# The RWKV stage of a two-layer trunk: VectorE's order written out by hand, substitutions and factors moved to other periods

## The chip, the cores and the metric

One core of a Trainium2 chip runs the whole program. The metric is the device time of one execution in microseconds (us); lower is better. About 0.5% of it, some 16 us, is what a measurement of this kernel can tell from no change.

## What is computed

The reference is a trunk of two layers (an MLA attention and a bidirectional RWKV side by side, then a mixture of experts), followed by a second block. The change touches only the RWKV part. For each of 8 heads and both directions it runs a recurrence over 528 positions with a 64 by 64 state:

```python
def step(S, inp):                       # one position
    r_t, w_t, k_t, v_t, kk_t, b_t = inp # b = kk * a
    sa = einsum('bhvk,bhk->bhv', S, kk_t)
    S = S * w_t[:, :, None, :] - sa[..., None] * b_t[:, :, None, :] + v_t[..., None] * k_t[:, :, None, :]
    return S, einsum('bhvk,bhk->bhv', S, r_t)

decay = exp(-exp(-softplus(-wl) - 0.5)); a = sigmoid(a0[d] + ad @ a2[d])
kd = k * (1 + (a - 1) * k_a)
y = scan(r, decay, kd, v, kk, a, reverse); bonus = sum(r * kd * r_k) * v
out = (group_norm(y_f + y_b) + bonus_f + bonus_b) * g
```

## The kernel before

The 528 positions (padded to 576) are cut into 9 chunks of 64. The work of a layer is 8 units: unit = (pair of heads, direction), two heads on the two halves of the 128 partitions. A unit passes through these steps, each a Python generator whose `yield`s are the places where other work may be put in between:

- **front** (L740): TensorE makes the two small products `sg` and `ta` (L764), ScalarE their tanh; GpSimd `sig` (L771), VectorE a running sum (L773), GpSimd its difference (L774), ScalarE three exponentials (L776 to L778). For a forward unit TensorE and VectorE first scale `kk` (L737, L738).
- **gen** (L787): VectorE multiplies the factors `KR` (L801, L805) and, with GpSimd, `BK` (L802 to L810) and, for a backward unit, the bonus factor (L852, L853); TensorE turns v (L884), makes the matrices Z of all chunks (L827) and turns BK (L842); VectorE masks Z (L830) and a DMA writes its triangular parts to DRAM (`Md`, L836).
- **inv** (L903): a DMA brings the 16 by 16 diagonal blocks back with one block per partition (`rnt`, L909); VectorE inverts them by substitution, 14 rounds of two small instructions (L914, L916); DMAs write the result out (`Td`, L922) and read it back in another layout (`rtb`, L927).
- **kx** (L983): transposes of KR (L884) and a product X (L993).
- **join** (L930): blocks of 16 are joined to 32 and to 64 by four rounds of TensorE and VectorE (L944 to L979). Its result T is what the next unit's solve reads.
- **solve** (L998): the products WC (L1006) and PG (L1017, added up on VectorE in L1018 and L1020), three groups of chunks each.
- **scan** (L1023): E and Y (L1036, L1050), then eight dependent steps, each two matmuls E (L1059), one VectorE scaling that writes the next state (L1060; L1052 before the first), and the output matmuls Y (L1062).
- **post** (L1078), for every finished pair of heads: group norm and gate; VectorE L1096, GpSimd L1102 and L1104, VectorE L1108.

`spread` deals several generators out in proportion to the number of steps that is given for each. `rwkv` (L1110) uses it: a prologue makes units 0 to 2 ready, then eight periods follow, one for each unit's solve and scan (the chain). Period i runs the chain of unit i, the join of unit i+1 inside the scan, and, spread over it, gen(i+2), kx(i+2) with inv(i+2), front(i+3), and in even periods from 2 on the post of an earlier pair.

The region is under `manual_schedule(engines={PE})`: TensorE issues in the order in which the program emits, while the order on VectorE, ScalarE, GpSimd and the DMA queue SP is chosen by a scheduler that works from a modelled timeline. Every engine issues its own queue in order. The pools named `rt`, `rbk`, `rnt` hold 7, 1 and 2 buffers.

Of the kernel before, what the change touches and what calls it, by code (L numbers as in the profile page):

```python
# [26 lines left out]
L = 528  # L27
# [76 lines left out]

# [6 lines left out]
class K:  # L111
# [503 lines left out]
    def rwkv_open(self, n):  # L615

        return (self.popen("rwl", dict(rl=(1, 1))),
                self.open("rwl", "left", dict(ryy=(LP, 2), rpt=(L, 2), rw2=(512, 3))),
                self.popen("rwp", dict(r=(1, 5), re=(1, 1), ry=(1, 1))),
                self.open("rw", "left", dict(  # L620
                    rq=(288, 2), rtb=(256, 3), rt0=(16, n), rtt=(LP, 2), rkx=(2 * LP, 2), rw=(LP, 1), rzb=(3 * LP, 2 * n),
                    rsv=(2 * LP, n), rkr=(2 * LP, n))),
                self.open("rg", "right", dict(rt=(LP, 7), rkk=(LP, 2), rkd=(L, 1), rbk=(2 * LP, 1), rpr=(56, 2), rnt=(256, 2), rsc=(LP, 1))))

# [47 lines left out]
    def rwkv_pre(self, li, u, rn):  # L672
# [67 lines left out]
    def rwkv_front(self, li, S, p, d, G):  # L740

        nc = self.nc
        par = S["par"]
        k = S["k"][p]
        if d == 0:
# [28 lines left out]
        nc.gpsimd.tensor_tensor(out=sig, in0=ai, in1=sig, op=ALU.subtract)  # L774
        eP, eE, eN = (self.t("rt", (128, LP)) for _ in range(3))
        nc.scalar.activation(out=eN, in_=ai, func=AF.Exp, scale=CDEC)  # L776
# [3 lines left out]
        nc.gpsimd.tensor_copy(al, c64(eP)[:, :, 63])  # L780
        G.update(p=p, d=d, al=al, ta=ta, eP=eP, eE=eE, eN=eN)
        yield

    def rwkv_gen(self, li, S, G):

        nc = self.nc
        p, d, ta, eP, eE, eN = (G[x] for x in ("p", "d", "ta", "eP", "eE", "eN"))  # L787
        par = S["par"]
        r, k, v, kk = S["r"][p], S["k"][p], S["v"][p], S["kk"][p]

# [3 lines left out]
        def rev(a):  # L794
            return a[:, :, ::-1] if d else a

        KR = self.t("rkr", (128, 2, NCH, 64))
        BK = S["BK"]
        b2 = self.t("rt", (128, LP))
        nc.vector.scalar_tensor_tensor(out=b2, in0=ta, scalar=1.0, in1=kk, op0=ALU.add, op1=ALU.mult)  # L800
        nc.vector.tensor_tensor(out=KR[:, 0], in0=rev(c64(kk)), in1=c64(eE), op=ALU.mult)  # L801
# [3 lines left out]
        nc.vector.tensor_tensor(out=KR[:, 1], in0=rev(c64(r)), in1=c64(eP), op=ALU.mult)  # L805
        for h in range(2):
            o = OWN[h]
            nc.vector.scalar_tensor_tensor(out=BK[o, :, h], in0=rev(c64(b2))[o], scalar=0.5, in1=c64(eN)[o], op0=ALU.mult,
                                           op1=ALU.mult)
            nc.gpsimd.tensor_tensor(out=BK[o, :, 1 - h], in0=rev(c64(ta))[o], in1=c64(eN)[o], op=ALU.mult)  # L810

        if d:
            vd = self.t("rt", (128, LP))
            nc.scalar.copy(rev(c64(vd)), c64(v))
        else:
            vd = v
# [20 lines left out]
        for c0, n in ((0, 5), (5, 4)):  # L837
# [7 lines left out]
            yield  # L845
        if d == 0:
            S["kd0"] = self.t("rkd", (128, L))
            nc.scalar.copy(S["kd0"], ta[:, PAD:])
        else:

            bs = S["kd0"]
            nc.gpsimd.tensor_tensor(out=bs, in0=bs, in1=ta[:, PAD:], op=ALU.add)  # L852
            nc.vector.scalar_tensor_tensor(out=bs, in0=r[:, PAD:], scalar=self.col(f"rk{li}", p), in1=bs, op0=ALU.mult,  # L853
                                           op1=ALU.mult)
        G.update(KR=KR, Zx=[z[:, :, 0] for z in ZB], BZ=[z[:, :, 1:3] for z in ZB], SV=SV)

    def rwkv_bonus(self, S, G):
        nc = self.nc
        bs, v = S["kd0"], S["v"][G["p"]]
        for c0, n in HALVES:  # L860
# [251 lines left out]
    def rwkv(self, li, u, rn, nb, freed):  # L1112
# [14 lines left out]
        def front(i):  # L1127
            if i <= last:
                yield from self.rwkv_front(li, S, *units[i], G[i])

        def gen(i):
            if i <= last:
                yield from self.rwkv_gen(li, S, G[i])
                inv = self.rwkv_inv(S, G[i])
                next(inv)
                if units[i][1]:
                    yield from self.rwkv_bonus(S, G[i])
                G[i]["inv"] = inv

        def back(i):  # L1140
            if i <= last:
                yield from spread((self.rwkv_kx(G[i]), 5), (G[i]["inv"], 7))
                if i == last:
                    self.close(hg)
                    freed()

        def join(i):
            if i <= last:
                yield from self.rwkv_join(S, G[i])

        def chain(i):
            yield from self.rwkv_solve(S, G[i])
            yield from spread((self.rwkv_scan(S, G[i]), 10), (join(i + 1), 4))

        with self.tc.manual_schedule(engines={ENG.PE}):
            run(spread((itertools.chain(front(0), gen(0), back(0)), 21), (front(1), 2)))
            run(spread((itertools.chain(gen(1), back(1)), 19), (front(2), 2)))
            run(spread((gen(2), 9), (join(0), 4)))
            for i in range(len(units)):
                behind = itertools.chain(gen(i + 2) if i else (), back(i + 2), front(i + 3))  # L1160
                p = i // 2 - 1
                post = self.rwkv_post(li, p, S, "r") if i % 2 == 0 and i else iter(())
                run(spread((chain(i), 20), (behind, 22), (post, 5)))
        self.close(hw)
# [1702 lines left out]
```

## Time and profile before

| | us |
|---|---|
| median of 3 runs | 3232.27 (3231.17 to 3242.57) |
| the profiled execution's own time | 3221.64 |
| its span | 3219.9 |
| RWKV of layer 0 in that span | 283.4 to 647.5 |
| RWKV of layer 1 in that span | 1374.1 to 1739.7 |

The span is what the trace covers; the time also holds what lies around it (1.7 us here). Times in the rows are counted from the span's start. A period begins with the first WC matmul (L1006) of its unit. A bracket at a row's end gives the idle time of that engine just before it and what ended it. PEclk is TensorE's granted clock as a share of 2.4 GHz, so 0.50 is 1.2 GHz.

### The profile page before, as it was taken

The page shows a single profiled execution, that of the slowest core. Times are in us where ns is not written, and L with a number is a line of the kernel's source. Part 1 is how long each engine was busy: PE and PEld are TensorE (multiplying, and loading weights), DVE is VectorE, ACT ScalarE, POOL GpSimd, SP SyncE. Part 2 cuts the span into 40 slices and gives each one's busy share as a digit, 9 for nine tenths or more (in the row PEclk, how much of TensorE's full clock was granted, in tenths as well). Part 3 has the DMA queues.
Part 4 walks back from the last instruction along what each step waited for, and adds up shares of the span by engine and source line. Part 5 has one row for each costly group of instructions (what it writes and reads, how often), then busy time and mean ns, then how long its engine had stood idle before and what let it go on. Part 6 is the DMA issues. An engine that isn't in the chain of part 4 may idle for free. (4 is left out here: it accounts for less than half of the span.)

```text
span 3219.9 us, 54694 instructions
## 1 busy us (share of the span) xinstructions
PE 2735.7 (85%) x21572; PEld 2085.6 (65%) x21572; DVE 1547.5 (48%) x3328; ACT 1086.0 (34%) x2377; POOL 1245.7 (39%) x1276
## 2 busy tenths in 40 slices
PE   6998777887789599967778788769888999999998
PEld 5887655664344288846557543248776788778886
DVE  6565545444124437664544611154867667344412
ACT  3223333311233322233332111144335665244431
POOL 3224222242244332341231511036865543655554
PEclk9997667787899799967778799989899999999999
DMA  5220111137989624311103599942121124523333
GB/s 186 63 86 20 19 16 16 61 133 304 364 344 374 249 69 148 90 29 19 16 13 123 199 361 420 420 173 92 55 76 43 61 71 130 156 87 97 98 119 104
DMA packets 224045, 443.18 MB, mean 138 GB/s; under 512 B 96577, under 2 KB 105153, under 8 KB 197137
## 3 DMA queue, kind: packets, MB, share of 16 engines
q1 hardware_dynamic: 209648, 407.76, 36.4%
q0 software_dynamic: 9216, 25.44, 2.1%
q10 hardware_dynamic: 4912, 6.34, 0.5%
q8 instruction: 175, 2.87, 0.4%
q14 instruction: 94, 0.76, 0.1%
HBM read 400.91 MB, written 46.61 MB: 139 GB/s over the span
## 5 line engine op out<-in xcount | busy, mean ns | idle before, releaser
L225 POOL TENSOR_TENSOR wl<-wr,wh 128x512 fp32r<-128x512 f32 x328 | 438.2, 1338 | 538.0 <-ACT wh L224 502.6
L224 ACT CAST wh<-wr 128x512 fp32r<-128x512 f32 x352 | 217.5, 619 | 552.0 <-PE mm L331 213.1
L330 PE MATMUL mm<-hh,wh 128*128 128x264 f32 x608 | 186.7, 307 | 19.1 <-ACT hf L285 13.0
L330 PE MATMUL mm<-h,wh 128*128 128x512 f32 x480 | 187.6, 391 | 2.5 <-ACT h L224 2.5
L332 PE MATMUL mm<-h,wl 128*128 128x512 f32 x480 | 187.5, 391 | 1.2 <-POOL wl L225 1.2
L331 PE MATMUL mm<-h,wh 128*128 128x512 f32 x480 | 187.4, 391 | 0.4 <-DVE h L225 0.4
L332 PE MATMUL mm<-hh,wl 128*128 128x264 f32 x608 | 181.4, 298 | 0.0
L331 PE MATMUL mm<-hl,wh 128*128 128x264 f32 x608 | 180.0, 296 | 0.0
L1455 POOL DMA_INDIRECT ybuf<-my,rdst x32 | 32.3, 1010 | 277.8 <-DVE my L1454 247.0
L330 PEld LDWEIGHTS mm<-hh,wh 128*128 128x128 f32 x608 | 119.0, 196 | 29.5 <-ACT hf L285 13.5
L330 PE MATMUL go<-h,wh 128*128 128x512 f32 x288 | 121.0, 420 | 11.6 <-ACT th L2139 6.8
L1426 DVE SCALAR_TENSOR_TENSOR mth<-mth,w 128x256 f32<-128x256 f32 x32 | 13.5, 421 | 236.0 <-ACT mth L1425 236.0
L331 PEld LDWEIGHTS mm<-hl,wh 128*128 128x128 f32 x608 | 119.1, 196 | 2.6 <-issue 1.3
L332 PEld LDWEIGHTS mm<-hh,wl 128*128 128x128 f32 x608 | 118.6, 195 | 2.3 <-issue 1.3
L1437 PE MATMUL w<-mw,xT 128*64 128x512 f32 x344 | 113.5, 619 | 5.5 <-DMA mw<-in_moe_w_dram 5.3
L332 PE MATMUL go<-h,wl 128*128 128x512 f32 x288 | 115.6, 401 | 0.0
L331 PE MATMUL go<-h,wh 128*128 128x512 f32 x288 | 115.2, 400 | 0.0
L1059 PE MATMUL E<-rzb,rkr 64*64 64x64 f32 x448 | 46.2, 296 | 80.9 <-DVE rzb L1060 54.5
L771 POOL TENSOR_SCALAR rt<-rt 128x576 f32<-128x576 f32 x16 | 10.8, 678 | 261.7 <-ACT rt L766 215.2
L219 POOL TENSOR_SCALAR rs<-s 128x4 f32<-128x4 f32 (+7 forms) x62 | 14.6, 236 | 236.1 <-DVE s L719 160.7
L330 PEld LDWEIGHTS mm<-h,wh 128*128 128x128 f32 x480 | 90.4, 188 | 21.4 <-ACT h L224 2.6
L332 PEld LDWEIGHTS mm<-h,wl 128*128 128x128 f32 x480 | 90.5, 189 | 20.7 <-POOL wl L225 2.1
(610 smaller groups left out, 7633.3 us busy)
## 6 DMA issues: line engine op xcount, KB each, us to landing
mw<-in_moe_w_dram SPq DMA_DIRECT2D x61, 1024.0 KB
mz<-in_moe_w_dram SPq DMA_DIRECT2D x48, 1024.0 KB
me<-in_moe_w_dram SPq DMA_DIRECT2D x47, 1024.0 KB
wr<-in_w_in_dram SPq DMA_DIRECT2D x176, 256.0 KB
mx<-in_moe_w_dram SPq DMA_DIRECT2D x36, 1024.0 KB
hf<-in_w_mod_dram SPq DMA_DIRECT2D x96, 256.0 KB
wr<-in_w_up_dram SPq DMA_DIRECT2D x88, 256.0 KB
wr<-in_w_down_dram SPq DMA_DIRECT2D x44, 256.0 KB
```

What stands on the lines that cost most here:

```text
L219: nc.gpsimd.tensor_scalar(out=a, in0=b, scalar1=float(mul), scalar2=float(eps), op0=ALU.mult, op1=ALU.add)
L224: self.nc.scalar.copy(hi, src)
L225: lo_eng.tensor_tensor(out=lo, in0=src, in1=hi.bitcast(F32), op=ALU.subtract)
L330: nc.tensor.matmul(out, lhsT=w[0], rhs=x[0], start=start, stop=False)
L331: nc.tensor.matmul(out, lhsT=w[0], rhs=x[1], start=False, stop=False)
L332: nc.tensor.matmul(out, lhsT=w[1], rhs=x[0], start=False, stop=stop)
L771: nc.gpsimd.tensor_scalar(out=rev(c64(sig)), in0=c64(sg), scalar1=0.5, scalar2=0.5, op0=ALU.mult, op1=ALU.add)
L1059: nc.tensor.matmul(o[OWN[h]], lhsT=P[OWN[h], c], rhs=St[OWN[h], c], start=False, stop=True, skip_group_check=True)
L1426: nc.vector.scalar_tensor_tensor(out=th, in0=th, scalar=1.0, in1=p[:, 0:256], op0=ALU.add, op1=ALU.mult)
L1437: nc.tensor.matmul(p1[q], lhsT=xT[:, kt, q], rhs=w13[kt // 4][:, kt % 4], start=kt == 0, stop=kt == 7)
L1455: nc.gpsimd.indirect_dma_start(out=ybuf, out_offset=bass.IndirectOffsetOnAxis(ap=dst, axis=0), in_=y, in_offset=None, bounds_check=2 * L - ...
```

## The change

1. The region's guard becomes `engines={PE, DVE}`: VectorE also issues in the order of emission.
2. Everything of a unit's factors but KR moves from gen to front: the products with `b2`, `ta`, the two halves of BK, the turned v (`vd`) and the bonus factor. They are made for unit i+3 in period i; gen(i+2) begins with KR alone. front gets `yield`s between its steps (8 steps in place of 1 or 2). `rbk` has 2 buffers instead of one shared one, `rt` 8 instead of 7.
3. inv runs a period later: period i holds inv(i+1), in its first third, and join(i+1) in its last 4 ninths. Before, inv(i+2) was in period i and the join in the scan.
4. The prologue is rearranged accordingly: it holds one substitution, inv(0), where before it held those of units 0 and 1.

```diff
-        S["BK"] = self.t("rbk", (128, NCH, 2, 64))      # one buffer, in rwkv_pre
 # rwkv_front: yields added behind sg, ta, sig and the running sum; behind the exponentials, moved from rwkv_gen:
+        nc.vector.scalar_tensor_tensor(out=b2, in0=ta, scalar=1.0, in1=kk, op0=ALU.add, op1=ALU.mult)
+        nc.gpsimd.tensor_scalar(out=ta, ...); nc.gpsimd.tensor_tensor(out=ta, in0=ta, in1=k, op=ALU.mult)
+        yield
+        BK = self.t("rbk", (128, NCH, 2, 64))           # both halves, VectorE and GpSimd; then vd
+        yield
+            nc.gpsimd.tensor_tensor(out=bs, in0=bs, in1=ta[:, PAD:], op=ALU.add)     # if d
+            yield
+            nc.vector.scalar_tensor_tensor(out=bs, in0=r[:, PAD:], scalar=self.col(f"rk{li}", p), in1=bs, ...)
 # rwkv
-        with self.tc.manual_schedule(engines={ENG.PE}):
-            run(spread((itertools.chain(front(0), gen(0), back(0)), 21), (front(1), 2)))
-            run(spread((itertools.chain(gen(1), back(1)), 19), (front(2), 2)))
-            run(spread((gen(2), 9), (join(0), 4)))
+        with self.tc.manual_schedule(engines={ENG.PE, ENG.DVE}):
+            run(front(0))
+            run(spread((gen(0), 8), (front(1), 9)))
+            run(spread((gen(1), 9), (itertools.chain(wait(2), inv(0)), 10), (front(2), 8)))
+            run(spread((gen(2), 8), (itertools.chain(kx(0), kx(1)), 10), (itertools.chain(wait(4), join(0)), 8)))
             for i in range(len(units)):
-                behind = itertools.chain(gen(i + 2) if i else (), back(i + 2), front(i + 3))
-                run(spread((chain(i), 20), (behind, 22), (post, 5)))
+                chain = itertools.chain(self.rwkv_solve(S, G[i]), self.rwkv_scan(S, G[i]))
+                behind = itertools.chain(gen(i + 2) if i else (), kx(i + 2), front(i + 3))
+                run(spread((chain, 17), (behind, 22 if i else 13), (itertools.chain(inv(i + 1), wait(18)), 27),
+                           (itertools.chain(wait(5), join(i + 1)), 9), (post, 5)))
```

`wait(n)` yields n times and does nothing: it only takes up places in the deal.

## Rows read from the trace of the kernel before

**Rows 1.** The page, part 1: busy time, share and instructions of each engine

```profile
PE 2735.7 (85%) x21572; PEld 2085.6 (65%) x21572; DVE 1547.5 (48%) x3328; ACT 1086.0 (34%) x2377; POOL 1245.7 (39%) x1276
```

**Rows 2.** Layer 0 by stretches: prologue, periods 0, 1, 2, 5, 6, 7

```profile
core 0: us, PE busy (x) PEld busy (x) DVE busy (x) ACT busy (x) POOL busy (x), PEclk, DMA share, GB/s
283.40:362.40 79.00, 51.83 (x524) 40.77 (x524) 50.82 (x111) 30.55 (x75) 30.58 (x29) 0.58 0.15 29
362.40:389.60 27.20, 22.34 (x454) 18.28 (x452) 15.64 (x53) 12.14 (x32) 9.92 (x10) 0.75 0.11 15
389.60:433.40 43.80, 34.16 (x523) 26.71 (x522) 20.34 (x66) 12.79 (x37) 0.81 (x2) 0.66 0.10 15
433.40:486.20 52.80, 39.71 (x542) 29.72 (x542) 26.93 (x76) 18.41 (x47) 20.10 (x20) 0.66 0.08 12
...
579.10:614.10 35.00, 26.55 (x509) 21.94 (x510) 16.28 (x59) 9.96 (x31) 6.10 (x5) 0.70 0.23 56
614.10:634.30 20.20, 19.26 (x425) 15.44 (x423) 9.34 (x29) 5.17 (x17) 5.50 (x7) 0.92 0.37 146
634.30:647.50 13.20, 11.30 (x204) 9.79 (x200) 5.35 (x17) 8.53 (x19) 1.05 (x2) 0.88 0.01 1
```

**Rows 3.** What TensorE waited for, layer 0, periods 1 to 7 (us in total, times, longest)

```profile
PE E L1059 <- DVE rzb L1060: 25.0, 22, 5.7
PE E L1059 <- DVE rzb L1052: 11.4, 5, 3.1
PE tok L884 <- ACT rt L814: 7.5, 2, 3.8
PE Z L827 <- POOL rbk L810: 6.8, 4, 2.7
```

**Rows 4.** The same of layer 1, periods 1 to 7

```profile
PE E L1059 <- DVE rzb L1060: 24.4, 24, 5.7
PE E L1059 <- DVE rzb L1052: 15.0, 5, 3.6
```

**Rows 5.** VectorE's queue in order of time, period 1: first product, then a scan step

```profile
408.91 0.17 DVE L914 TENSOR_TENSOR rpr<-rnt 72x14 f32<-72x14 f32 x1 [5.25 <-DMA rnt<-Md]
...
415.99 0.27 DVE L1060 TENSOR_SCALAR rzb<-E,s 128x64 f32<-128x64 f32 x1
...
422.50 0.45 DVE L944 STREAM_TRANSPOSE rq<-rtb 128x256 f32<-128x256 f32 x1 [1.83 <-DMA rtb<-Td]
```

**Rows 6.** TensorE's queue in order of time: scan steps of periods 1 and 7

```profile
416.31 0.48 PE L1059 MATMUL E<-rzb,rkr 64*64 64x64 f32 x4 [5.74 <-DVE rzb L1060]
...
643.59 0.33 PE L1059 MATMUL E<-rzb,rkr 64*64 64x64 f32 x4 [0.27 <-DVE rzb L1060]
```

**Rows 7.** Stretches within period 2: in and after the gap

```profile
460.00:462.00 2.00, 0.48 (x3) 0.49 (x4) 1.79 (x9) 0.00 (x0) 0.00 (x0) 0.50 0.00 0
462.00:480.00 18.00, 16.25 (x234) 11.57 (x234) 7.68 (x26) 4.59 (x12) 3.98 (x5) 0.50 0.10 13
```

**Rows 8.** SP's queue: the write of period 1's inverted blocks

```profile
416.10 1.69 SPq L922 DMA_DIRECT2D Td<-rnt  x2
```

**Rows 9.** GpSimd's queue: a backward unit's factors (period 0), a post (period 2)

```profile
377.86 0.67 POOL L771 TENSOR_SCALAR rt<-rt 128x576 f32<-128x576 f32 x1 [26.46 <-ACT rt L766]
...
388.44 1.30 POOL L852 TENSOR_TENSOR rkd<-rkd,rt 128x528 f32<-128x528 f32 x1
...
469.12 1.18 POOL L1102 TENSOR_SCALAR ryy<-ryy,pv 128x264 f32<-128x264 f32 x1 [13.25 <-DVE ryy L1096]
470.38 0.74 POOL L1104 TENSOR_TENSOR ryy<-ryy,u 128x264 f32<-128x264 f32 x1
```

**Rows 10.** VectorE's queue in the prologue: bonus factor, one substitution step beside GpSimd

```profile
307.97 0.77 DVE L853 SCALAR_TENSOR_TENSOR rkd<-ur,pv,rkd 128x528 f32<-128x528 f32 x1 [1.28 <-POOL rkd L852]
...
340.52 1.42 DVE L916 TENSOR_TENSOR rnt<-rnt,rpr 72x54 f32<-72x54 f32 x1
```

**Rows 11.** GpSimd's queue at that place

```profile
340.46 1.41 POOL L774 TENSOR_TENSOR rt<-rt,rt 128x576 f32<-128x576 f32 x1 [1.88 <-DVE rt L773]
```

More of the change, by code (lines that the diff above doesn't have):

```diff
@@ L102, in spread, with wait @@
             continue
+        yield
+def wait(n):
+    for _ in range(n):
         yield
@@ L743, in rwkv_front @@
         par = S["par"]
-        k = S["k"][p]
+        r, k, v = S["r"][p], S["k"][p], S["v"][p]
         if d == 0:
@@ L780, in rwkv_front @@
         nc.gpsimd.tensor_copy(al, c64(eP)[:, :, 63])
[L781 to L789, printed above, removed]
-        def c64(t):
-            return t.rearrange("p (c t) -> p c t", t=64)
[L794 to L798, printed above, removed]
         b2 = self.t("rt", (128, LP))
+        kk = S["kk"][p]
         nc.vector.scalar_tensor_tensor(out=b2, in0=ta, scalar=1.0, in1=kk, op0=ALU.add, op1=ALU.mult)
-        nc.vector.tensor_tensor(out=KR[:, 0], in0=rev(c64(kk)), in1=c64(eE), op=ALU.mult)
         nc.gpsimd.tensor_scalar(out=ta, in0=ta, scalar1=par[:, 16 + p:17 + p], scalar2=par[:, 20 + p:21 + p],
@@ L804, in rwkv_gen @@
         nc.gpsimd.tensor_tensor(out=ta, in0=ta, in1=k, op=ALU.mult)
-        nc.vector.tensor_tensor(out=KR[:, 1], in0=rev(c64(r)), in1=c64(eP), op=ALU.mult)
+        yield
+        BK = self.t("rbk", (128, NCH, 2, 64))
         for h in range(2):
@@ L816, in rwkv_gen, with c64, rev @@
             vd = v
+        yield
+        if d == 0:
+            S["kd0"] = self.t("rkd", (128, L))
+            nc.scalar.copy(S["kd0"], ta[:, PAD:])
+        else:
+            bs = S["kd0"]
+            nc.gpsimd.tensor_tensor(out=bs, in0=bs, in1=ta[:, PAD:], op=ALU.add)
+            yield
+            nc.vector.scalar_tensor_tensor(out=bs, in0=r[:, PAD:], scalar=self.col(f"rk{li}", p), in1=bs, op0=ALU.mult,
+                                           op1=ALU.mult)
+        G.update(p=p, d=d, al=al, eP=eP, eE=eE, BK=BK, vd=vd, bs=S["kd0"])
+        yield
+    def rwkv_gen(self, li, S, G):
+        nc = self.nc
+        p, d, eP, eE, BK = (G[x] for x in ("p", "d", "eP", "eE", "BK"))
+        r, kk = S["r"][p], S["kk"][p]
+        def c64(t):
+            return t.rearrange("p (c t) -> p c t", t=64)
+        def rev(a):
+            return a[:, :, ::-1] if d else a
+        KR = self.t("rkr", (128, 2, NCH, 64))
+        for i, (x, e) in enumerate(((kk, eE), (r, eP))):
+            nc.vector.tensor_tensor(out=KR[:, i], in0=rev(c64(x)), in1=c64(e), op=ALU.mult)
         SV = self.t("rsv", (128, NCH, 2, 64))
-        yield from self.by_token(vd, SV[:, :, 0], SV[:, :, 1], True)
+        yield from self.by_token(G["vd"], SV[:, :, 0], SV[:, :, 1], True)
         ZB = [self.t("rzb", (128, NCH, 3, 64)) for _ in range(2)]
@@ L845, in rwkv_gen @@
             yield
[L846 to L854, printed above, removed]
         G.update(KR=KR, Zx=[z[:, :, 0] for z in ZB], BZ=[z[:, :, 1:3] for z in ZB], SV=SV)
@@ L858, in rwkv_bonus @@
         nc = self.nc
-        bs, v = S["kd0"], S["v"][G["p"]]
+        bs, v = G["bs"], S["v"][G["p"]]
         for c0, n in HALVES:
@@ L1127, in front @@
         def front(i):
-            if i <= last:
-                yield from self.rwkv_front(li, S, *units[i], G[i])
+            return self.rwkv_front(li, S, *units[i], G[i]) if i <= last else iter(())
         def gen(i):
@@ L1133, in gen, with kx, inv @@
                 yield from self.rwkv_gen(li, S, G[i])
-                inv = self.rwkv_inv(S, G[i])
-                next(inv)
                 if units[i][1]:
                     yield from self.rwkv_bonus(S, G[i])
-                G[i]["inv"] = inv
-        def back(i):
+        def kx(i):
+            return self.rwkv_kx(G[i]) if i <= last else iter(())
+        def inv(i):
             if i <= last:
-                yield from spread((self.rwkv_kx(G[i]), 5), (G[i]["inv"], 7))
+                yield from self.rwkv_inv(S, G[i])
                 if i == last:
@@ L1147, in join @@
         def join(i):
[L1148 to L1153, printed above, removed]
-        with self.tc.manual_schedule(engines={ENG.PE}):
-            run(spread((itertools.chain(front(0), gen(0), back(0)), 21), (front(1), 2)))
-            run(spread((itertools.chain(gen(1), back(1)), 19), (front(2), 2)))
-            run(spread((gen(2), 9), (join(0), 4)))
-            for i in range(len(units)):
-                behind = itertools.chain(gen(i + 2) if i else (), back(i + 2), front(i + 3))
-                p = i // 2 - 1
-                post = self.rwkv_post(li, p, S, "r") if i % 2 == 0 and i else iter(())
-                run(spread((chain(i), 20), (behind, 22), (post, 5)))
+            return self.rwkv_join(S, G[i]) if i <= last else iter(())
+        with self.tc.manual_schedule(engines={ENG.PE, ENG.DVE}):
[3 more added lines that the diff above has]
+            run(spread((gen(2), 8), (itertools.chain(kx(0), kx(1)), 10), (itertools.chain(wait(4), join(0)), 8)))
+            for i in range(len(units)):
+                chain = itertools.chain(self.rwkv_solve(S, G[i]), self.rwkv_scan(S, G[i]))
+                behind = itertools.chain(gen(i + 2) if i else (), kx(i + 2), front(i + 3))
+                post = self.rwkv_post(li, i // 2 - 1, S, "r") if i % 2 == 0 and i else iter(())
+                run(spread((chain, 17), (behind, 22 if i else 13), (itertools.chain(inv(i + 1), wait(18)), 27),
+                           (itertools.chain(wait(5), join(i + 1)), 9), (post, 5)))
         self.close(hw)
```

3 lines of the change are left out of this document (2 added, 1 removed).

## The prediction

> **What bounds the kernel now.** I read the page's busy times first: TensorE is busy 85% of the span, VectorE 48% [rows 1]. That average hides the RWKV stage, so I cut the stage into its periods with the view by stretches. The two layers spend 364 and 366 us in it. In layer 0 the prologue is 79.0 us long with TensorE busy for 51.8; period 1 43.8 with 34.2; period 2 52.8 with 39.7; period 5 35.0 with 26.6 [rows 2]. So TensorE, the busiest engine here too, stands idle for about a quarter of each, and its granted clock is 0.58 to 0.75; only periods 6 and 7, which have no unit behind them to prepare, come to 0.92 and 0.88 [rows 2].
>
> Then I asked what ended TensorE's idle time. From period 1 on, 36.4 us of layer 0 went to scan steps (L1059) that waited for VectorE's scaling, and 14.3 us to the front's tail: the turned v (L814) and BK (L810) [rows 3]. Layer 1 has 39.4 us of the first kind [rows 4]. The queue of VectorE shows why the scan waits. In period 1 the first substitution instruction begins at 408.91, after 5.25 us on its DMA, with the scan's first scaling queued behind it; the next scaling comes at 415.99, when all 14 rounds are done [rows 5]. TensorE's step waits 5.74 us for it [rows 6]. VectorE is not full: it issues in a bad order.
>
> **Part 1, the substitution out of the scan's way.** The 28 instructions are spread over the solve, where TensorE has over 13 us of products queued. Nothing of them is left in the scan, whose own handshake remains: 0.27 us a step in period 7 [rows 6], some 5 us over periods 1 to 5. Of 36.4 and 39.4 us, 7 more belong to periods 6 and 7 and to short waits that stay; I take 29 us a layer as removed. The load's wait goes too, since Md was written a period earlier; what hides it is that whole period. Bounds: 20 to 34.
>
> **Part 2, the factors a period ahead.** The waits for BK and the turned v, 14.3 us, vanish, because they are done before the period starts [rows 3]: -14 us a layer (bounds -10 to -14).
>
> **Part 3, the prologue.** One substitution with its round trip leaves it. A substitution took 415.99 - 408.91 = 7.1 us [rows 5], and from the write at 416.10 to the first instruction that uses the read-back at 422.50 pass 6.4 us [rows 5, 8]. These 13.5 us lie partly beside unit 2's factors, so I take -10 us (bounds -3 to -18).
>
> **Part 4, the clock.** In period 2 the clock was 0.50 in the gap, and stayed there through the next 18 us though TensorE was busy for 16.3 of them [rows 7]. A scan step's matmul then lasts 0.48 us, against 0.33 in period 7, which keeps 0.88 with its 0.27 us gaps [rows 2, 6]. Without the long gap the second half of a period should stay at 2.4 GHz where no new gap comes. In periods 1 and 3 some 17 us at half clock would shrink by 5, in period 5 by 2: -12 us a layer (bounds 0 to -25; the even periods get a new gap, below).
>
> By the Trainium skill, TensorE: Matmul & The Clock Gate, section "A second HAM failure mode: psum-queue depth-cycling", frequent micro-idles between groups of matmuls are enough to make the clock swing. Period 7's 0.88 with a gap in every step speaks against that here; by the page this term would be nil.
>
> **Part 5, what is added.** VectorE now waits in its queue wherever the emission has it wait. Three places count.
> - *Periods 2 and 4, the bonus factor.* They make a backward unit's factors. L853 stands just ahead of L979, the join's last copy, on which the next WC waits. L853 needs GpSimd's L852. From L771 to the end of L852 GpSimd takes 389.74 - 377.86 = 11.9 us, and a post's two instructions add 1.18 + 0.74 [rows 9], with L1108 waiting for them in the same VectorE queue. With L853's 0.77 [rows 10] and a copy or two T is ready some 15.5 us after L771. TensorE's work emitted behind that place is about a third of the period: 13 us at half clock (a third of 39.7 [rows 2]), 8.5 at full. So it stands idle 2.5 to 7 us; I take 5, twice: +10. L771 itself can't slip, since its inputs come in TensorE's order.
> - *L1108 behind L1096.* In post's other half VectorE waits 1.9 us for GpSimd with scan steps queued behind: about 1 us each in periods 2, 4 and 6: +3. In periods 1 and 3 the running sum, b2 and BK stand between the last scan steps: about 2.5 us each, an estimate between nothing and the 5 us of these instructions: +5.
> - *Period 6.* It was 20.2 us long with unit 7's join ready to start [rows 2]. Now it holds inv(7) too: some 10 us until the last piece, then the 6.4 us round trip [rows 5, 8], then join and half the scan, about half of TensorE's 19.3 us [rows 2], together 26: +7 with the clock falling.
>
> Together +25 us a layer (bounds +10 to +45). The moved instructions keep their durations; the extra DMA places on SP are the same DMAs later, hidden since Td's write (1.69 us to issue [rows 8]) has a third of a period to go. The weights of the next stage, loaded when unit 7's inv ends, come some 15 us later and still over 20 us ahead of their use; without that cover they would cost those 15.
>
> **Sum.** -29 - 14 - 10 - 12 + 25 = -40 us a layer, -80 for two. The profiled execution took 3221.64 us (span 3219.9), so 3141.6 by its own time; it lies 10.6 below the median, and the same -80 from the median 3232.27 gives **3152**.
>
> **Rivals.**
> - *Faster: the clock holds everywhere* and GpSimd finishes sooner, as it would if VectorE stands still beside it. Additions at +10, clock at -25: -68 a layer, **3096**. For it: period 6's 0.92 [rows 2]. Against: GpSimd's 11.9 us chain is of mostly undisturbed instructions. Chance 0.15.
> - *The clock gains nothing*, as the page has it: -28 a layer, **3176**. Chance 0.09.
> - *GpSimd holds up the pieces.* In the prologue L916, 0.2 us elsewhere, took 1.42 us beside GpSimd's L774 of 1.41, and ended with it [rows 10, 11]. After an odd period GpSimd still works on BK while the next substitution begins. Six such stretches cost VectorE 7 us in the first third, of which TensorE's queue covers 4 or 5: some +2.5 us in six periods, -25 a layer, **3182**. The Trainium skill, SBUF — State Buffer, section "Who interferes with whom", says a VectorE instruction with two SBUF inputs contends with a GpSimd one that reads SBUF, and the loser waits for the whole instruction; the row agrees, and it speaks against this change. Chance 0.08.
> - *GpSimd ends the even periods.* If TensorE is ahead at full clock and the post's GpSimd work queues behind the factors twice, periods 2 and 4 lose 15 instead of 5 us, the clock term goes (12), and posts wait 2 us more often (4): -4 a layer, **3224**. Chance 0.08.
> - *Slower: the join waits for the read-back in every period.* L944 stands ahead of scan steps 4 to 8 in VectorE's fixed order, and its Q matmul ahead of theirs in TensorE's. If the pieces end less than 6.4 us before the scan's third step, all of that stops. The price is period 6's 7 us in six more periods, and the clock term: -40 + 42 + 12 = +14 a layer, **3260**. Against: a third of a 35 us period is 12 us, the round trip ends at 19, the join begins at 21; that is 2 us of slack, no more. Chance 0.07.
> - *It does not do what it says*: the load L909 is issued late, so VectorE's first instruction of each period waits for it as now (5.25 us [rows 5]) with all else behind. About no change, **3228**. Chance 0.03.
>
> **How the numbers follow.** The forecast, 3152 (own range 3127 to 3177), has 0.50. Faster by over 0.5% (below 3216) collects it and the first three rivals: 0.82; within 0.5% the fourth and the last: 0.11; slower 0.07. The range reaches from just under the fast rival to the late-load case, 3090 to 3228; that leaves out the slow rival and half of what is faster than the fast one.
>
> **What would show it.** Right: no wait of L1059 over 2 us in odd periods; no wait for L810 or L814; 28 products and sums all before L1052 of the chain; periods 1 and 3 at 33 to 37 us, 2 and 4 at 42 to 47, 6 at 25 to 28; VectorE waiting for L852 at the end of even periods. Wrong: L944 waiting for its DMA in all periods with L1059 behind; a granted clock in periods 1 to 5 that stays at 0.70 although the gaps are gone; L914 and L916 at over 0.4 us mean; a prologue still near 79 us.

## The result and the profile after

The changed kernel takes **3193.03 us** (3186.1 to 3194.76), the kernel before 3231.72 with the four runs taken beside it: a ratio of 0.9872, 95% interval 0.9842 to 0.9903. That is 1.3% faster, with an interval clear of no change: the way that was forecast and inside the range, but by 39 us where 80 were forecast. The profiled executions show 3186.1 (span 3184.2) against 3221.64, 35.5 us.

First the RWKV stage by periods, layer 0: prologue, then periods 0 to 7 (it answers to [rows 2] and has its columns).

```profile
279.60:348.40 68.80, 48.86 (x514) 38.33 (x516) 44.23 (x81) 29.48 (x75) 28.83 (x29) 0.63 0.14 31
348.40:377.20 28.80, 20.85 (x470) 16.66 (x464) 17.33 (x55) 12.43 (x33) 10.06 (x10) 0.80 0.10 12
377.20:412.50 35.30, 29.73 (x525) 23.19 (x524) 21.41 (x66) 14.81 (x39) 3.44 (x6) 0.79 0.12 18
412.50:458.10 45.60, 34.38 (x544) 26.10 (x543) 28.38 (x72) 16.76 (x44) 20.59 (x21) 0.76 0.09 14
458.10:499.40 41.30, 32.57 (x523) 25.33 (x522) 22.29 (x68) 14.03 (x38) 5.06 (x8) 0.71 0.10 16
499.40:546.50 47.10, 36.58 (x544) 27.77 (x543) 27.90 (x73) 16.75 (x44) 20.49 (x19) 0.72 0.09 14
546.50:580.10 33.60, 25.78 (x509) 21.06 (x508) 18.44 (x63) 9.81 (x30) 1.68 (x2) 0.75 0.12 19
580.10:611.90 31.80, 26.49 (x423) 19.96 (x419) 14.34 (x58) 5.75 (x17) 6.60 (x9) 0.66 0.41 146
611.90:627.20 15.30, 13.60 (x204) 11.73 (x200) 4.99 (x16) 8.07 (x18) 0.12 (x1) 0.72 0.01 2
```

Two things are to be read from such a row. Its length less TensorE's busy time is the time in which TensorE stood idle. And where two kernels have the same products in a stretch, a difference in busy time is put down to the clock. The stage went from 364.1 to 347.6 us in layer 0 (TensorE busy 276.4 to 268.8, idle 87.6 to 78.8) and from 365.7 to 341.7 in layer 1 (busy 269.1 to 258.6, idle 96.6 to 83.1): 40 us, some 18 by the clock and 22 by idle time. Period by period, in us:

| | prologue | 0 | 1 | 2 | 3 | 4 | 5 | 6 | 7 |
|---|---|---|---|---|---|---|---|---|---|
| layer 0 before | 79.0 | 27.2 | 43.8 | 52.8 | 41.4 | 51.5 | 35.0 | 20.2 | 13.2 |
| layer 0 after | 68.8 | 28.8 | 35.3 | 45.6 | 41.3 | 47.1 | 33.6 | 31.8 | 15.3 |
| layer 1 before | 82.5 | 27.9 | 42.8 | 50.9 | 41.1 | 51.1 | 35.9 | 20.3 | 13.3 |
| layer 1 after | 70.9 | 28.9 | 32.1 | 44.6 | 37.0 | 46.8 | 33.1 | 33.1 | 15.2 |

Outside the stage the span changed by -3.8 us ahead of it, -2.6 between the layers and +11.2 behind the second, where nothing is edited; other kernels below show 1485 to 1494 us for that last part (before: 1480). What does that was not tested; part of it can be the one profiled execution of the kernel before, which lies 10 us under that kernel's median.

Then what TensorE waited for in periods 1 to 5 of layer 0 (it answers to [rows 3]; us in total, times, longest). These lines add up to 43.7 us, the idle time of those five rows being 43.9: what TensorE waited for there is all in this list.

```profile
PE Y L1072 <- DVE rzb L1070: 9.6, 5, 2.8
PE WC L1016 <- DVE rtt L989: 9.0, 4, 2.3
PE PG L1027 <- DVE rzb L849: 6.3, 8, 1.1
PE Q L959 <- DVE rq L954: 5.3, 3, 1.9
PE E L1069 <- DVE rzb L1070: 5.1, 7, 2.1
PE Q L979 <- ACT rt L784: 4.2, 2, 2.1
PE Q L979 <- DVE rq L974: 1.8, 3, 0.6
PE hs L718 <- DVE rzb L849: 1.4, 2, 0.7
PE Q L959 <- ACT rkx L1004: 0.8, 2, 0.4
PE U L967 <- issue: 0.2, 1, 0.2
```

The scan step's wait for its scaling, L1069 now, has gone from 33.8 us in these periods to 5.1, and the waits for BK and the turned v are gone altogether. In their place stand waits that had no line before: for the scan's last product (L1072), for the join's last copy (L989), for the masks (L849), and inside the join (L959, L979). All but 5.2 us are for VectorE. They end in its queue, here at the end of period 2 in layer 0 (VectorE, then GpSimd; a release in brackets).

```profile
451.29 0.43 DVE L982 COPY rq<-Q 32x256 f32<-32x256 f32 x1 [2.60 <-ACT rq L981]
451.73 3.55 DVE L798 SCALAR_TENSOR_TENSOR rbk<-rt,rt 64x576 f32<-64x576 f32 x2
455.31 0.28 DVE L1070 TENSOR_SCALAR rzb<-E,s 128x64 f32<-128x64 f32 x1
455.51 0.48 DVE L1106 SCALAR_TENSOR_TENSOR ryy<-ryy,pv,hb 128x264 f32<-128x264 f32 x1
459.92 0.43 DVE L1118 TENSOR_TENSOR ur<-ryy,g 128x264 f32<-128x264 f32 x1 [3.93 <-POOL ryy L1114]
460.27 0.76 DVE L815 SCALAR_TENSOR_TENSOR rkd<-ur,pv,rkd 128x528 f32<-128x528 f32 x1
461.06 0.42 DVE L989 COPY rtt<-U 32x256 f32<-32x256 f32 x1
...
452.86 3.68 POOL L800 TENSOR_TENSOR rbk<-rt,rt 64x576 f32<-64x576 f32 x2
456.62 1.30 POOL L813 TENSOR_TENSOR rkd<-rkd,rt 128x528 f32<-128x528 f32 x1
457.90 1.16 POOL L1112 TENSOR_SCALAR ryy<-ryy,pv 128x264 f32<-128x264 f32 x1
459.15 0.74 POOL L1114 TENSOR_TENSOR ryy<-ryy,u 128x264 f32<-128x264 f32 x1
```

The last scaling of the scan stands behind BK (3.55 us), and the join's last copy behind GpSimd's whole chain. BK's two halves lie beside GpSimd's product ahead of BK (L793) and its own two halves, and took 3.55 us together. Over the whole program (duration in ns: shortest, median, longest), the kernel before first:

```profile
L808 DVE SCALAR_TENSOR_TENSOR rbk<-rt,rt x32: 741/755/1854, 292.7 to 1669.2; 64x576 f32<-64x576 f32 x32
```

```profile
L798 DVE SCALAR_TENSOR_TENSOR rbk<-rt,rt x32: 740/1764/1961, 286.7 to 1606.8; 64x576 f32<-64x576 f32 x32
```

The Trainium skill, SBUF — State Buffer, section "Who interferes with whom", says that a VectorE instruction with two SBUF inputs contends with a GpSimd one that reads SBUF, for ports under an exclusive lock; these rows fit it. The prediction's rival had GpSimd strike the substitution in the periods. There no piece ran beside a GpSimd instruction, so that was not put to the test: the pieces have a median of 0.20 us. In the two prologues seven of them did meet GpSimd's work and took 0.64 to 1.47 us. In the periods it is BK that was struck.

### The profile page after: what moved, and what is told of

It is laid out like the page before. It is cut to its first block, busy times and chain, and to the rows that moved or that the text cites. A ratio compares the mean times of both kernels' runs of the same rounds, so it can differ in the third digit from the quotient of the medians.

```text
span 3184.2 us, 54720 instructions
## 1 busy us (share of the span) xinstructions
PE 2716.5 (85%) x21572; PEld 2070.2 (65%) x21572; DVE 1559.3 (49%) x3328; ACT 1085.6 (34%) x2377; POOL 1231.7 (39%) x1276
## 5 line engine op out<-in xcount | busy, mean ns | idle before, releaser
L335 PE MATMUL go<-h,wh 128*128 128x512 f32 x288 | 121.1, 420 | 13.1 <-ACT th L2145 8.7
L224 POOL TENSOR_SCALAR rs<-s 128x4 f32<-128x4 f32 (+7 forms) x62 | 14.7, 238 | 273.4 <-DVE s L723 196.0
L335 PEld LDWEIGHTS mm<-h,wh 128*128 128x128 f32 x480 | 90.5, 189 | 21.2 <-ACT h L229 2.5
L336 PEld LDWEIGHTS mm<-h,wh 128*128 128x128 f32 x480 | 90.5, 189 | 19.4 <-issue 0.6
L1652 DVE SCALAR_TENSOR_TENSOR ma<-hf,sc,ma 128x512 f32<-128x512 f32 x112 | 94.5, 862 | 17.5 <-DMA hf<-in_w_mod_dram 16.8
```

The costliest lines, as they stand in the source:

```text
L335: nc.tensor.matmul(out, lhsT=w[0], rhs=x[0], start=start, stop=False)
L336: nc.tensor.matmul(out, lhsT=w[0], rhs=x[1], start=False, stop=False)
L1652: nc.vector.scalar_tensor_tensor(out=a, in0=w, scalar=sc[:, kt, c:c + 1], in1=a, op0=ALU.mult, op1=ALU.add)
```

## The experiments

All edits are to the changed kernel unless said otherwise. Ratios are to the kernel before on the same chip; a stage length is the sum over both layers in the profiled execution (before 729.8 us, changed kernel 689.3).

**1. VectorE's order left to the scheduler.**

```diff
-        with self.tc.manual_schedule(engines={ENG.PE, ENG.DVE}):
+        with self.tc.manual_schedule(engines={ENG.PE}):
```

> The changed kernel with its emission untouched, but VectorE's order left to the scheduler again (only TensorE's order is laid down). Theory A, the order is what gains: the scheduler lines up the 28 instructions of a substitution in a row, and does so ahead of the additions to P and G and of the scan's scalings, so a stall of about 7 us comes back in most of periods 0 to 5: +20 to +45 us a layer, 3235 to 3280 us in all, with TensorE's waits for the scaling and for the additions at over 25 us a layer (changed kernel: 8). Rival B, the place in the program is what gains, since with the substitution a period behind its matrices nothing waits for it: within 10 us of the changed kernel's 3193.

3202.49 us, ratio 0.9922 (0.9894 to 0.995), 10 us over the changed kernel; stage 705.0. B, at its edge: most of the gain needs no order by hand. The waits that A names did come back in part (L1069 in periods 1 to 5 of layer 0: 25.0 us, where the changed kernel has 5.1), yet the idle time of these periods is 41.4 us, less than the changed kernel's 43.9, since other waits are smaller (those for the join's last copy 3.2 us). The two ratios' intervals just overlap, so what the order by hand adds is small. The order by hand is better in periods 0 and 1 of layer 0 (28.8 and 35.3 against 33.1 and 39.8 us) and worse in periods 2, 4 and 6 (45.6, 47.1 and 31.8 against 41.9, 42.5 and 25.1). Periods 2 and 6 under the scheduler:

```profile
427.80:469.70 41.90, 35.30 (x544) 26.49 (x543) 24.83 (x71) 16.15 (x43) 17.09 (x18) 0.74 0.10 16
591.70:616.80 25.10, 23.04 (x422) 17.52 (x420) 9.17 (x28) 5.76 (x17) 6.42 (x8) 0.77 0.36 144
```

**2. The kernel before, its VectorE order laid down as emitted** (the same line, the other way).

> The kernel before with nothing moved, but VectorE's order laid down as emitted. Theory A, order and place are both needed: the first round of a substitution then stands in VectorE's queue right behind its own matrices, so the queue stops for the load's 5 us (rows 5) with scan steps behind it, and the join's first transpose stops it for the round trip; 5 to 10 us in each of periods 0 to 5, against some 30 us a layer of scan waits that go: 3215 to 3290 us, and TensorE's scan waits remain over 20 us a layer. Rival B, the order alone gives most of it: 3180 to 3205.

3237.25 us, ratio 1.0021 (1.0006 to 1.0035): A in the time, with 18.6 us of scan waits in layer 0, a little under what A asked for. The order alone gains nothing: period 1 falls to 39.3 us, but period 6 grows to 29.4 and the prologue to 79.6 (layer 1 87.0).

**3. The factors made in the unit's own gen again**, all else as changed.

```diff
 def rwkv_front(...):
-        b2 = ...; BK = ...; vd = ...; bs = ...
 def rwkv_gen(...):
+        b2 = ...; BK = ...; vd = ...
         KR = ...
...
+        bs = ...
```

> The changed kernel with one part undone: b2, the two halves of BK, the turned v and the bonus factor are made in the unit's own gen again, as before, all else as changed. Theory A (my forecast's parts 2 and 5): the 14 us of waits for BK and the turned v return, while GpSimd's work leaves the tail of even periods (5 us each, +10 a layer given back): +2 to +14 us a layer, 3197 to 3221 us; periods 3 and 5 longer by 3 to 6 us, periods 2 and 4 the same or shorter. Rival C, moving the factors cost more than it gained: 3165 to 3190.

3186.48 us, ratio 0.9864 (0.9842 to 0.9885); stage 688.1. The median lies in C's range, but the ratio cannot be told from the changed kernel's 0.9872; A is out. The move of the factors is worth nothing that can be measured. Periods 1 and 4 of layer 0:

```profile
379.10:419.00 39.90, 32.81 (x523) 25.71 (x522) 25.82 (x66) 14.81 (x39) 10.40 (x10) 0.71 0.10 16
505.10:548.10 43.00, 33.33 (x542) 25.67 (x541) 27.64 (x75) 16.77 (x44) 15.97 (x16) 0.82 0.10 16
```

Period 1 is 4.6 us longer and period 4 4.1 shorter than changed; in layer 1 it is 4.8 and 4.1. Periods 3 and 5 lengthen by 0.5 to 2.4, under A's 3 to 6. The waits for BK and the turned v came back as 7.2 us in layer 0 (14.3 in the kernel before), and those at the periods' ends fell from 18.6 to 4.8; other waits took up the rest, so that idle time in periods 1 to 5 is 42.5 us.

Here BK is back at a median of 0.756 us, and its rows show why. Both halves run beside GpSimd's L806, which scales `ta` and has one tensor for input, and it is this instruction that is long, 1.97 us where it takes 0.82 in the changed kernel (L791):

```profile
420.11 1.52 DVE L812 SCALAR_TENSOR_TENSOR rbk<-rt,rt 64x576 f32<-64x576 f32 x2
...
420.18 1.97 POOL L806 TENSOR_SCALAR rt<-rt,rpar 128x576 f32<-128x576 f32 x1 [2.18 <-DVE rt L805]
```

VectorE's two products of KR follow beside GpSimd's next work and take 1.12 and 1.95 us.

**4. The substitution beside its own unit's kx again**, in pieces, the rest as changed.

```diff
# prologue
-  run(spread((gen(2), 8), (itertools.chain(kx(0), kx(1)), 10), ...
+  run(spread((gen(2), 8), (itertools.chain(kx(0), spread((kx(1), 5), (inv(1), 8))), 18), ...
# periods
-  behind = itertools.chain(gen(i + 2) if i else (), kx(i + 2), front(i + 3))
+  behind = itertools.chain(gen(i + 2) if i else (), spread((kx(i + 2), 5), (inv(i + 2), 8)), front(i + 3))
-  run(spread((chain, 17), (behind, 22 if i else 13), (itertools.chain(inv(i + 1), wait(18)), 27), ...
+  run(spread((chain, 17), (behind, 30 if i else 21), ...
```

> The changed kernel with one part undone: the substitution is emitted beside the kx of its own unit, in the period that makes its matrices, as before, in pieces; the factors stay a period ahead and VectorE's order stays laid down. Theory A (forecast's part 1 and 3): VectorE's queue stops for the load (5 us) in each period and a substitution comes back into the prologue: +20 to +40 us a layer, 3233 to 3275 us; prologue back at 76 to 82 us, period 6 back at 20 to 24 us. Rival D, the pieces between scan steps hide the load as well: within 10 us of 3193, with period 6 shorter by 10 and the others longer by no more than that.

3226.96 us, ratio 0.9996 (0.9986 to 1.0007): with this one part undone the whole gain is gone, 6 us short of A's range. But how it goes is not A's. The prologue stays at 69.8 us although a substitution is back in it, and period 6 is 25.9. In periods 1 to 5 of layer 0 TensorE is idle for 46.4 us, 2.5 more than changed, but busy for 173.6 against 159.0 with the same products; in layer 1 idle 43.0 against 42.2, busy 171.9 against 151.4. So the place of the substitution buys clock. It does not bring the old scan waits back: L1069 has 12.4 us here (kernel before: 33.8), and the largest wait is another:

```profile
PE WC L1016 <- DVE rtt L989: 11.6, 4, 5.6
```

Period 1 here, and then two stretches of it:

```profile
383.90:425.50 41.60, 34.73 (x525) 26.53 (x524) 21.12 (x67) 13.63 (x37) 5.11 (x5) 0.66 0.10 16
...
404.70:408.86 4.16, 1.00 (x49) 0.89 (x53) 3.12 (x16) 0.33 (x2) 0.00 (x0) 0.72 0.00 0
408.86:425.50 16.64, 15.58 (x265) 11.47 (x257) 7.62 (x23) 5.20 (x11) 1.84 (x2) 0.50 0.11 16
```

and the last stretch of period 1 in the changed kernel:

```profile
400.73:412.50 11.77, 9.10 (x168) 6.54 (x166) 5.92 (x11) 5.28 (x11) 3.44 (x6) 0.50 0.01 1
```

With pieces between the scan's first steps TensorE is busy for only 1.00 of 4.16 us in the middle of the period, falls to 1.2 GHz there (granted clock 0.72 in this stretch), and the remaining 16.6 us run at 0.50; in the changed kernel the fall comes later and 11.8 us do. The gap alone does not settle it: in layer 1 TensorE is busy for 1.01 of 3.46 us at the same place, the clock falls to 0.65 behind it and is back at 1.00 some 7 us later, and the period is 34.6 us long. Of the 20.4 us of busy time by which layer 1 is over the changed kernel in periods 1 to 5, 8.6 lie in period 2 (42.2 us, changed 33.6).

**5. The post's two GpSimd instructions as one on VectorE.**

```diff
-            if p == 3:
+            if True:
                 nc.vector.scalar_tensor_tensor(out=y[:, q], in0=y[:, q], scalar=self.col(f"gnb{li}", p), in1=v[:, q], op0=ALU.add,
                                                op1=ALU.add)
```

> The changed kernel with the post's two GpSimd instructions (add gnb, add v) replaced by one VectorE instruction for every pair, as it is for the last one. Theory A, GpSimd's tail holds up even periods: VectorE's 16.4 us of waits for the post's GpSimd sum in layer 0 (six waits of 2.1 to 3.9 us, with scan steps or the join's last copies queued behind) are gone for six instructions of about 0.45 us; periods 2 and 4 shorter by 3 to 5 us each, period 6 by 2 to 4: 3167 to 3177 us in all. Rival B, these waits lie under TensorE's queue or under the bonus factor, which needs GpSimd at the same place: within 5 us of 3193.

3173.4 us, ratio 0.9825 (0.9787 to 0.9864): A in the time. VectorE's waits for the post's sum are gone, and TensorE's idle time in periods 1 to 5 falls from 43.9 to 35.8 us in layer 0 and from 42.2 to 35.4 in layer 1. The wait for the join's last copy is gone behind periods 2 and 4 (2.3 us each, at the start of periods 3 and 5) and stays behind periods 1 and 3 (2.2 each); the scan's last product still waits 2.8 and 2.0 us in periods 2 and 4. The clock follows unevenly: the stage loses 15 us in layer 0 and 3 in layer 1. Periods 2 and 4 lose 1.6 and 4.2 us in layer 0, and in layer 1 change by +1.5 and -0.7, where A had 3 to 5 less for each; period 6 loses only 1.0 and 0.5, where A had 2 to 4.

**6. Unit 7's substitution in period 5.**

```diff
-  behind = itertools.chain(gen(i + 2) if i else (), kx(i + 2), front(i + 3))
+  behind = itertools.chain(gen(i + 2) if i else (), kx(i + 2), (inv(7) if i == 5 else ()), front(i + 3))
-  ... (itertools.chain(inv(i + 1), wait(18)), 27) ...
+  ... (itertools.chain(inv(i + 1), wait(18)) if i != 6 else iter(()), 27) ...
```

> The changed kernel with one substitution moved: unit 7's stands in period 5, behind its own matrices and kx, not in period 6; the other units as changed. Theory A, period 6 is as long as the last substitution's chain (10 us of pieces, 6 us round trip, then the join): period 6 back to 20 to 23 us and period 7 to 13.3 to 14, period 5 longer by 1 to 4: -8 to -11 us a layer, 3171 to 3177 us. Rival B, period 6 is long for its clock (0.65, before 0.92) and the post's waits, whatever the substitution does: period 6 not under 28 us, within 6 us of 3193.

3188.39 us, ratio 0.9874 (0.9844 to 0.9904). The time is B's, and its ratio cannot be told from the changed kernel's; period 6 lies between the two theories: it is 26.8 us, in layer 1 27.9, so the substitution accounts for 5 of the 12 us by which it had grown, not all. The rest shows in its rows: a scan step waits 2.05 us for VectorE, which waits for the post's GpSimd sum, and the last part runs at 0.50.

```profile
604.44 0.43 DVE L1118 TENSOR_TENSOR ur<-ryy,g 128x264 f32<-128x264 f32 x1 [2.14 <-POOL ryy L1114]
605.11 0.28 DVE L1070 TENSOR_SCALAR rzb<-E,s 128x64 f32<-128x64 f32 x1
...
605.45 0.33 PE L1069 MATMUL E<-rzb,rkr 64*64 64x64 f32 x4 [2.05 <-DVE rzb L1070]
...
609.00:612.00 3.00, 3.00 (x41) 1.83 (x42) 0.49 (x1) 0.59 (x1) 1.90 (x2) 0.50 0.00 0
```

**7. Filling matmuls where TensorE waits in the join.**

```diff
# self.fill() is called behind the join's first transpose (L954) and behind its last copy (L989)
+    def fill(self):
+        ps = self.pa("fill", "r")
+        for _ in range(3):
+            self.nc.tensor.matmul(ps[:, :256], lhsT=self.ident, rhs=self.pv[:, :256], start=True, stop=True)
```

> The changed kernel with work added that nobody reads: three matmuls of 256 columns on TensorE ahead of each join's first product and at each join's end, where TensorE waits for VectorE (1.9 to 2.3 us each in the changed kernel). They cover these waits, so TensorE is not idle there. Theory A, it is these gaps that lose the clock: the granted clock of periods 2 to 6 rises from 0.65 to 0.78 to over 0.80, period 3 of layer 0 (41.4 us) comes to layer 1's 37 and period 6 falls by 2 to 5 us: 3165 to 3185 us. Rival B, the clock follows the whole mix of waits: clock within 0.04 of the changed kernel's, and the fillers cost what they take where nothing waits, 0 to 8 us a layer: 3190 to 3210.

3183.85 us, ratio 0.9847 (0.982 to 0.9874). The clock part of A holds for the most part: 0.92 in period 3 and 0.88 in period 5 of layer 0, where the changed kernel has 0.71 and 0.75, and period 3 is 35.7 us; period 2 has 0.77.

```profile
462.00:497.70 35.70, 29.89 (x535) 23.47 (x534) 24.50 (x69) 14.17 (x39) 5.89 (x8) 0.92 0.12 18
543.00:574.30 31.30, 27.11 (x521) 21.89 (x520) 19.40 (x72) 10.17 (x31) 0.00 (x0) 0.88 0.13 21
574.30:606.50 32.20, 25.15 (x432) 18.93 (x431) 13.40 (x50) 5.76 (x17) 6.72 (x9) 0.81 0.41 144
```

But these matmuls are some 4.4 us of work in each period, period 6 did not fall in layer 0 (31.0 against 33.1 in layer 1), and even periods hardly did (period 2: 45.6). The median is 9 us lower, in A's range, with an interval that overlaps the changed kernel's. By the Trainium skill, TensorE: Matmul & The Clock Gate, section "A second HAM failure mode: psum-queue depth-cycling", frequent micro-idles between groups of matmuls make the clock swing. The prediction set period 7's 0.88 [rows 2, 6] against that. In the changed kernel the scan steps of period 7 bear the page out: their gaps are 0.3 us at most (1.7 in all), and yet the clock falls once more after it had risen, to a mean of 0.72. The second half of period 7 there, in two parts:

```profile
619.60:623.40 3.80, 3.26 (x92) 2.79 (x88) 1.43 (x6) 3.80 (x6) 0.00 (x0) 1.00 0.02 4
623.40:627.20 3.80, 2.64 (x38) 1.92 (x36) 1.36 (x5) 1.34 (x3) 0.00 (x0) 0.72 0.00 0
```

**8 and 9. Edits together.** First the factors in gen with edits 5 and 6:

> Three edits to the changed kernel together: the factors made in gen again, the post on VectorE, and unit 7's substitution in period 5. If the three effects add (0 to -7 for the factors, -16 to -26 for the post, -16 to -22 for the substitution): 3138 to 3177 us. If one bound takes the place of another: 3175 to 3195.

3180.18 us, ratio 0.9839 (0.9803 to 0.9875), not below edit 5 alone: the effects do not add. Then edits 5, 6 and 7 with the factors left ahead:

> Three edits to the changed kernel together, the factors left a period ahead: the post on VectorE, unit 7's substitution in period 5, and the filling matmuls of 256 columns. Measured singly they gave -20, -5 and -9 us. Theory A, they are different causes and add: 3153 to 3167 us; period 6, which held the substitution, the post's wait and a low clock at once, comes back to 20 to 24 us (23.5 before less what the fillers take) in both layers. Rival B, they fill the same gaps: 3167 to 3180, period 6 at 25 or more.

3173.64 us, ratio 0.9834 (0.9811 to 0.9857): B in both. Period 6 is 26.4 and 28.0 us; it has 1.5 us of idle time left, so its length is work at a clock of 0.82 and 0.74.

**10. BK, the turned v and the bonus factor emitted behind the join**, on top of 9.

```diff
-  behind = itertools.chain(..., front(i + 3))
+  f = front(i + 3)
+  behind = itertools.chain(..., until_cut(f))      # up to the piece ahead of BK; how f marks it is left out here
   run(spread((chain, 17), ..., (post, 5)))
+  run(f)
```

> The kernel of e9_sum with one more edit: of the front's factors the last two steps (BK, the turned v, the bonus factor) are emitted behind the join of the period instead of beside its last scan steps, so that the join's last copy stands ahead of BK's 2.9 us in VectorE's queue. Theory A, the order at the end of a period is what is late: TensorE's waits for the join's last copy and for the last scaling (9.0 and 9.7 us in layer 0 of the changed kernel) fall under 4 us each, periods 1 to 4 shorter by 1 to 4 us: -6 to -16 us a layer against e9_sum. Rival B, VectorE is the bound at the start of a period (its masks are already late, 6.3 us of waits of the products for P and G): 2.9 us more ahead of the masks cost as much there: within 5 us of e9_sum, the waits for masks over 10 us a layer; or slower by up to 10.

3151.51 us, ratio **0.9765** (0.9745 to 0.9785), the lowest of all: A, -22 us on 9. The scan's last product waits 7.1 us in periods 1 to 5 of layer 0 where it was 13.1 in 9 (A had under 4), and the masks cost no more (3.0 against 3.6). The join's last copy is not among what TensorE waits for, but nor is it in 9, where the filling matmuls stand in its place. In layer 0 periods 2 and 4 come to 40.3 and 40.8 us (44.4 and 44.3 in 9) and period 0 to 27.4 (30.3); the odd ones gain nothing, where A had 1 to 4 us less for 1 and 3 too (33.9, 38.1 and 33.9, in 9 34.0, 33.5 and 32.7). Periods 1 to 5 of layer 0, the line of 9, then the largest waits here, then period 6:

```profile
PE Y L1079 <- DVE rzb L1077: 13.1, 5, 3.8
...
PE Y L1082 <- DVE rzb L1080: 7.1, 5, 2.3
PE Q L983 <- ACT rt L784: 4.0, 2, 2.1
PE Z L849 <- DVE ryy L1103: 3.3, 2, 1.6
PE Q L983 <- DVE rq L978: 3.3, 3, 1.8
PE PG L1037 <- DVE rzb L852: 3.0, 3, 1.4
...
565.00:588.60 23.60, 22.08 (x434) 17.02 (x433) 10.74 (x32) 5.76 (x17) 2.70 (x4) 0.93 0.55 197
```

Idle time in periods 1 to 5 is 27.0 us, in 9 32.1; in both some 22 us of filling matmuls count as busy. BK still takes a median of 1.77 us, but nobody waits for it there.

**11 and 12. The join's half copies on VectorE instead of ScalarE**, on top of 9, then on top of 10.

```diff
-        nc.scalar.copy(Q[q4(1)], ps[q4(1), :8])
+        nc.vector.tensor_copy(Q[q4(1)], ps[q4(1), :8])
-        nc.scalar.copy(T[q4(0), 1:9, 32:64], ps[q4(0), :8])
+        nc.vector.tensor_copy(T[q4(0), 1:9, 32:64], ps[q4(0), :8])
```

> The kernel of e9_sum with one more edit: in the join the half copies that ScalarE makes of Q and of the last block (two instructions a unit) are made by VectorE beside their other halves. In the changed kernel VectorE waits 1.3 to 2.6 us for ScalarE at each of these (12.0 us in layer 0, six times), with scan steps queued behind. Theory A, ScalarE's exponentials delay the join: -1 to -2 us in each of periods 1 to 6, -6 to -12 us a layer against e9_sum. Rival B, VectorE's two more instructions (0.43 us each) and the products' own time take up what is saved: within 4 us a layer.

> The kernels of e10_bk_behind_join and e11_halves_on_vector together: the changed kernel with the post on VectorE, unit 7's substitution in period 5, the filling matmuls, the front's last two steps behind the join, and the join's half copies on VectorE. Against e9_sum (3174) the fourth gave -22 us and the fifth -7. Theory A, the fifth shortens the join wherever it stands, so they add: 3140 to 3148 us. Rival B, with BK behind the join the join's end is no longer what TensorE waits for (its waits for the last copy are gone in e10), so the fifth gives nothing more: 3149 to 3156 us.

3166.32 us, ratio 0.9803 (0.9778 to 0.9828): the stage is 3 and 7 us shorter than in 9, which does not settle it. On top of 10: 3158.01 us, ratio 0.978 (0.9759 to 0.9801), no gain over 10: nearest to B, 2 us above its range. (The stage is 3 us shorter than in 10, 639.4 against 642.5, the rest of the span 8 longer.) The lowest time is that of 10, 2.35% under the kernel before, where the changed kernel is 1.28% under it; 10 and 12 cannot be told apart.

## Why the prediction was right, and half too high

Its terms for one layer beside what the two profiles show, idle time taken from the rows of waits and clock from TensorE's busy time (us):

| | forecast | layer 0 | layer 1 |
|---|---|---|---|
| prologue (part 3) | -10 | -10.2 | -11.6 |
| period 0 | 0 | +1.6 | +1.0 |
| periods 1 to 5: scan waits (part 1) | -29 | -28.7 | -31.8 |
| periods 1 to 5: factors' waits (part 2) | -14 | -14.3 | -13.2 |
| periods 1 to 5: waits at the periods' ends (part 5) | +17 | +17.0 | +17.5 |
| periods 1 to 5: waits not foreseen | 0 | +17.2 | +14.7 |
| periods 1 to 5: clock (part 4) | -12 | -12.7 | -15.5 |
| periods 6 and 7 (part 5) | +8 | +13.7 | +14.8 |
| sum | -40 | -16 | -24 |

**What held.** The waits removed, the clock of periods 1 to 5 and the waits at the periods' ends came out within 4 us of their terms. The ends are the lines of L1072 and L989 (9.6 + 9.0, less 1.6 that the latter had before). The mechanism for even periods is as described, GpSimd's chain with the post behind it: edit 5 takes the post out of it, and the wait of 2.3 us for the join's last copy goes.

**Sums that came out by luck.** Inside two of these terms the parts are not those forecast. The ends cost 5.1 and 4.3 us in layer 0 at periods 2 and 4, for which 5 each was forecast, and 4.3 each at periods 1 and 3, for which 2.5 was an estimate; the 1 us each for scan steps behind the post's other half is in L1069's line (2.1 each, 0.5 in edit 5). The clock's 12 us were to come in periods 1, 3 and 5, and the even periods to gain none; TensorE's busy time in layer 0 fell by 4.7 us in the odd periods and by 8.0 in periods 2 and 4 (layer 1: 10.2 and 5.3).

**The step that failed: "What is added. Three places count."** There are five. The masks of gen stand behind a substitution's pieces in VectorE's queue and TensorE's P and G products wait for their PSUM behind them (L849: 6.3 + 1.4). And the join, whose steps on VectorE the scheduler placed before, now has a fixed place in both queues: its first product waits for VectorE's transpose of the read-back (L959, 5.3 + 0.8), its second for ScalarE's exponentials or VectorE (L979, 4.2 + 1.8). That is 19.8 us, less 2.6 of small waits that went. The slower rival had named the join's wait for the read-back, with 7 us a period; in layer 0 VectorE waited 1.2 to 1.5 us for it, three times in periods 1 to 5.

**Period 6** was put at 25 to 28 us and came to 31.8 and 33.1. Its start is the one forecast (last piece 11 us after the period's start, read-back used 5.7 later), but the clock was sized too low: of the 11.6 us in layer 0 4.4 are idle time and 7.2 busy time at a lower clock (0.66, before 0.92), and period 7, forecast at no change, begins at 0.50 and costs 2 more (clock 0.72, before 0.88). Edit 6 gives the substitution 5 of it; with the post, the fillers and BK's place also changed (edit 10) period 6 has 1.5 us of idle time and a clock of 0.93.

**Right number, wrong reason.** The prologue's 10 us are not the substitution taken out of it: edit 4 puts one back and stays at 69.8 and 71.6. They go with the new interleaving of the prologue, which edits 3 and 4 share (69.3 and 73.4 in edit 3), and some 5 to 7 of them with VectorE's order in it, since edit 1 has 73.6 and 77.7; the order alone, in edit 2, gains none. Which piece of the interleaving does it was not tested. And part 1's 29 us of scan waits do vanish, but what they cost by themselves no run shows. Undoing the move (edit 4) brings 12.4 us of them and other waits, in all 2.5 and 0.8 us more idle time in periods 1 to 5, but 14.6 and 20.4 us more busy time at the same products. **"The moved instructions keep their durations"** was wrong too: BK's halves went from 0.755 to 1.764 us. And part 2's 14 us were real but bought nothing (edit 3): the same instructions went to the end of a period, where the scan's last step and the join stood behind them, and TensorE waited 18.6 us for these two in layer 0 (4.8 in edit 3).

## What to carry to other kernels

When a queue is laid down by hand, a removed wait is only half of the sum: list every instruction that now stands behind a moved one, and ask at each period's end what the last copy on the critical chain is queued behind. Here moving work earlier by a period gained nothing when it was emitted ahead of that copy (edit 3), and putting it behind gained 22 us (edit 10 on 9); the factors in gen with all of 9's other edits were not run. Account for idle time and for busy time at equal work apart, for a placement can be paid almost entirely in clock (edit 4).

## What the runs showed of the hardware

- The same instructions in the same order take 41.3 us in period 3 of layer 0 and 37.0 in layer 1: in layer 0 a wait of 1.9 us (0.3 in layer 1) at the join's first product comes before a fall to 1.2 GHz that lasts to the period's end (granted clock of the period 0.71 against 0.78).
- TensorE filled for 4.4 us a period with work that nobody reads ended sooner, since period 3 then ran at 0.92: 35.7 us instead of 41.3, with 12 more matmuls in it.
- VectorE's BK half has a median of 0.755 us in the kernel before and in edit 1, 0.756 in edit 3, 1.76 in the changed kernel, 1.77 in edit 10 and 1.84 in edit 2. Which of the two engines pays depends on what meets: beside GpSimd's products VectorE's half was long, beside its L806, which has one tensor for input, GpSimd's instruction was (1.97 us for 0.82, edit 3).
- Not every pair meets so: in period 2 of edit 4 ten instructions of a substitution took 0.18 to 0.21 us each while GpSimd's L225 was under way (8 columns in 1.69 us, then 2 in 0.74).
